# Six k-tiles of an output projection as three pairs of seven block products, in one column part of 1024

## The chip, the cores and the metric

One core of one Trainium2 chip runs one decoder layer in float32. The metric is the device time of one execution in microseconds; the median of several executions counts. TensorE is called PE in the profile, its weight loads PEld, VectorE DVE, ScalarE ACT, GpSimd POOL; SyncE (SP) only issues loads and stores.

## What is computed

A layer with 256 tokens and a model width of 2048. Two groups of eight attention heads give `mixed` (256 x 2048); the change lies in the projection that follows, and what comes behind it reads the projection's result:

```python
mixed = jnp.concatenate([a_out.reshape(B, S, DSWA_HEADS * HEAD_DIM),
                         b_out.reshape(B, S, MLA_HEADS * V_HEAD_DIM)], axis=-1)
x = x + _rmsnorm(mixed @ w_out[layer], norm_attn_post[layer])

h = _rmsnorm(x, norm_mlp_pre[layer])
u = jnp.square(jax.nn.relu(h @ w_up[layer]))
x = x + _rmsnorm(u @ w_down[layer], norm_mlp_post[layer])
```

`w_out` is 2048 x 2048, `w_up` 2048 x 8192, `w_down` 8192 x 2048.

## The kernel before

**Products of three.** A float32 operand is used as two parts, hi (rounded, made by ScalarE) and lo (the rest, made by VectorE as `source - hi`). A product is three matmuls onto one accumulator: hi x hi, hi x lo, lo x hi. The activations are the stationary side (128 x 128, one k-tile of 128 rows and one block `b` of 128 tokens), the weights the moving side, 512 columns wide. `mm` at line 304 issues them. There are NB = 2 token blocks and KD = 16 k-tiles.

**Weights.** `Weights` holds a list of weight tiles in the order of use. For each, SP loads a raw tile (up to 128 x 1024 floats, five raw buffers, line 198), then ScalarE makes hi and VectorE lo (`split`, lines 314 and 315; with a gain 318 and 319), in eight pairs of buffers. When the matmuls ask for tile i, the work for all tiles up to i + `ahead` is put out; `ahead` is 6 (`W_AHEAD`) and 4 (`AHEAD_NORM`) around the norm behind the output projection. So the order of the loads and splits in each engine's queue is fixed when the program is built.

**The order of side work.** `Flow` keeps a clock of the matmuls put out so far. Side work (norms, attention heads, evacuations) is written as generators that yield delays in microseconds; `flow.pump()` puts out what is due. `flow.until` and `flow.finish` put it out early where data are needed. Engines run their own queues in order and wait for each other by semaphores.

**The output projection.** `mixT` holds `mixed` transposed, hi and lo, k-tiles 0 to 7 from the first head group and 8 to 15 from the second. The 2048 columns are four parts of 512 (`ch_o`), each with eight weight tiles of two k-tiles. Parts 0 and 1 are interleaved, while the last heads finish; then part 2, then part 3, where the last `APART[0]` = 5 tiles (10 k-tiles) are done for token block 0 first and then for block 1. Part 2 and part 3 take 16 x 2 x 3 = 96 matmuls each. When an accumulator is complete, `out_evac` squares it on ScalarE for the norm (line 897) and multiplies it by the gain on VectorE (`yg`, line 898). At the end of parts 0 and 1 the pools of the attention are given up, the gain `g_post` and `x` are loaded, and `powers` starts: four squares of `g_post` (line 915), a few steps on 128 x 2 elements (lines 917 to 926), and four scalings of `x` (line 931).

**The residual and the next projection.** After part 3 of a token block, `residual(b)` reduces the squares, takes the root on GpSimd (line 506), updates `x` in four pieces (line 943), and transposes each piece on TensorE (`ht`, line 308); ScalarE and VectorE split it into `hT` (hi and lo). The up projection's first column part (j = 0) takes its first `APART[1]` = 7 k-tiles for block 0 and then for block 1: its 42 matmuls on block 0 lie ahead of the first that needs block 1.

**Seven products.** The later column parts of the up projection, and the down projection, already do some pairs of k-tiles otherwise. A pair of k-tiles, two token blocks and two halves of 512 columns make a 2 x 2 by 2 x 2 product of blocks, which takes eight block products of three matmuls, 24 in all; by sums of blocks it takes seven, 21 matmuls (`seven_products`). That needs, on the weights' side, two sums `t` and `u` of the pair's raw tiles on VectorE (lines 366 to 371; four adds of 512 where the two k-tiles lie in separate raw tiles), so that a pair has hi and lo of four operands, one 512 wide (`b11`) and three 1024 wide, in place of two. On the activations' side it needs four sums of blocks, split into hi and lo (`four_sums` at line 1111 does them in three instructions). Of the seven products three go straight onto the accumulators and four onto accumulators `m` of their own; after the last pair `close` (line 1175) forms what is to be added from those, by a copy on ScalarE and four VectorE instructions in a chain (line 1181), and one VectorE add for each accumulator (line 1243) ends it. `three_more` issues three matmuls onto an accumulator that such an add has changed.

Of the kernel before, what the change touches and what calls it, by code (L numbers as in the profile page):

```python
# [26 lines left out]
P = 128  # L27
D = 2048
# [48 lines left out]
APART = (5, 7)  # L77
# [37 lines left out]

THREE = up_steps(range(6, 11), (11, 12), (13,), (14, 15))
# [155 lines left out]
def layer(nc, tc, io):  # L272
    flow = Flow()

    def pool(name, side, **kw):
        return tc.alloc_tile_pool(name=name, bufs=1, side=side, **kw)
# [144 lines left out]
    wide_u, after = [], 0  # L421
# [547 lines left out]
    def heads_done(k, b):  # L969
        if k >= HA:  # L970
            flow.until(lambda: k - HA in made)
# [3 lines left out]

    res = [None] * NB
    for ns in ((0, 1), (2,), (3,)):
        if len(ns) == 2:
            order = [(c, t, b) for ts in (range(4), range(4, 6), range(6, 8)) for c in range(2) for t in ts for b in range(NB)]
        else:  # L980
            order = [(0, t, b) for t, b in in_order(8, (0, APART[0] if ns == (3,) else 0))]
        for c, b, acc in proj(mixT, [ch_o[n] for n in ns], f"o{ns[0]}", order, heads_done):
            n = ns[c]
            if not late:
                flow.finish(*workers)
                pb.release()
                lat.release()
                hp = pool("hp", "left")
                late["hT"] = [hp.tile([P, KD, S], F32R, name=f"hT_{w}") for w in ("hi", "lo")]
                po = late["po"] = pool("po", "right")  # L990
                late["g_post"] = po.tile([P, D], F32, name="g_post")
                nc.sync.dma_start(out=late["g_post"],
                                  in_=io["norm_attn_post"].partition_broadcast(P).rearrange("p o d -> p (o d)"))
                late["yg"] = [po.tile([P, D], F32, name=f"yg{b}") for b in range(NB)]
                for b_ in range(NB):
                    xs.append(po.tile([P, D], F32, name=f"x{b_}"))
                    nc.sync.dma_start(out=xs[b_], in_=io["x"][b_ * P:(b_ + 1) * P, :])
                pw_chain = flow.start(powers())
            out_evac(n, b, acc[0])
            if n == 3:  # L1000
                flow.finish(pw_chain)
                weights.ahead = AHEAD_NORM
                res[b] = flow.start(residual(b), b * D_SECOND)
                flow.pump()
# [106 lines left out]
    def four_sums(q, f):  # L1111

        tt = nc.vector.tensor_tensor
        fs, qs = [x.rearrange("p (k s) -> p k s", s=P) for x in (f, q)]
        tt(out=qs[:, 0:2], in0=fs[:, 0:2], in1=fs[:, 1:4:2], op=OP.subtract)
        tt(out=qs[:, 2], in0=qs[:, 0], in1=fs[:, 3], op=OP.add)
        tt(out=qs[:, 3], in0=fs[:, 2], in1=qs[:, 2], op=OP.subtract)

# [35 lines left out]
    def three(out, a, w, first, last):  # L1154

        for i, (x, y) in enumerate(((0, 0), (0, 1), (1, 0))):
            mm(out, a[x], w[y], first and i == 0, last and i == 2)

    def seven_products(ts, left, accs, m, first, last, m_first=False):

        (a11, a12, a22), (s3, s1, s2, s4) = left
        prods = ((a11, 0, 0, 1), (a12, 1, 0, (0, 0)), (s4, 1, 1, (0, 1)), (s2, 2, 0, 6), (a22, 2, 1, (1, 0)),
                 (s3, 3, 1, 7), (s1, 3, 0, 5))
        if m_first:
            prods = sorted(prods, key=lambda x: not isinstance(x[3], int))
        for p, (a, i, half, to) in enumerate(prods):
            w = weights.get(ts[i])
            in_m = isinstance(to, int)
            three(m[to] if in_m else accs[to], a, [w[x][:, half * 512:half * 512 + 512] for x in range(2)],
                  in_m and first, in_m and last)  # L1170
            if all(x[1] != i for x in prods[p + 1:]):
                weights.free(ts[i])
            flow.pump()

    def close(c, m):

        tt = nc.vector.tensor_tensor
        nc.scalar.activation(c[0], m[1], AF.Copy)
        for out, x, y, op in ((1, m[6], c[0], OP.subtract), (2, m[7], c[1], OP.subtract),
                              (3, m[5], c[2], OP.subtract), (1, m[5], c[1], OP.add)):  # L1180
            tt(out=c[out], in0=x, in1=y, op=op)
        return dict(zip(PARTS, c))

# [3 lines left out]
    PARTS = ((0, 0), (0, 1), (1, 0), (1, 1))  # L1187
# [121 lines left out]
    def half_evac(more, g_half):  # L1309
# [7 lines left out]
        for b, n in order:  # L1317
# [3 lines left out]
            yield 1.0  # L1321

    added = [False]

    def three_more(out, a, w):

        for x, z in ((0, 0), (0, 1), (1, 0)):
            nc.tensor.matmul(out, a[x], w[z], start=False, stop=(x, z) == (1, 0), skip_group_check=True)  # L1328
            flow.spend(MM)
# [130 lines left out]
```

## Time and profile before

| | us |
|---|---|
| median of 3 runs (lowest to highest) | 1025.0 (1021.83 to 1026.27) |
| profiled execution | 1022.25 |
| its span, first to last instruction | 1020.5 |
| PE busy in the span | 1010.1 |
| DVE, ACT, POOL busy | 839.3, 624.3, 94.0 |
| first matmul of column part 2, first of the up projection | 296.8, 341.25 |

The span is 1.75 us shorter than the execution's own time. Rows of the timeline give start, duration, engine, line, instruction, and in brackets the idle time of that engine before it with what ended it. A matmul's duration (0.39) is from its issue to its end; they overlap, so the pace is read from the starts. The row of a stage gives the busy time of each engine in it.

### The profile page before, as it was taken

How to read it: one execution, taken by the hardware profiler on the slowest of the kernel's cores; microseconds unless marked ns; L12 is line 12 of the kernel's file. 1: busy time of each engine (PE TensorE's matmuls, PEld its weight loads, DVE VectorE, ACT ScalarE, POOL GpSimd, SP SyncE). 2: the span in 40 equal slices, each digit the busy share in tenths (PEclk: the TensorE clock that was granted, in tenths of full speed). 3: DMA queues.
4: the chain of work that ended last, by engine and by line, in shares of the span. 5: the costliest groups of instructions: out<-in, count | busy, mean ns of one | idle time of the engine just before them, and what ended most of it. 6: DMA issues, size and time to landing. Idle time of an engine off the chain costs nothing.

```text
span 1020.5 us, 13280 instructions
## 1 busy us (share of the span) xinstructions
PE 1010.1 (99%) x4678; PEld 842.9 (83%) x4678; DVE 839.3 (82%) x1125; ACT 624.3 (61%) x822; POOL 94.0 (9%) x148
## 2 busy tenths in 40 slices
PE   9999999999999999999999999999999999999996
PEld 6888889898888788888888888888888888888885
DVE  6677747676656779998999989898999989898896
ACT  6575437555463567566766776676666665767571
POOL 0020202002101000000010100000110000211100
PEclk9999999999999999999999999999999999999999
DMA  8977759556686298778988979579989866988972
GB/s 291 373 253 260 251 162 313 175 165 192 201 306 210 89 385 247 259 257 242 298 258 283 286 221 301 190 254 365 344 263 385 301 226 235 326 309 293 320 258 82
DMA packets 108370, 266.02 MB, mean 261 GB/s; under 512 B 9488, under 2 KB 28432, under 8 KB 107664
## 3 DMA queue, kind: packets, MB, share of 16 engines
q1 hardware_dynamic: 65488, 177.24, 51.3%
q0 software_dynamic: 19440, 68.17, 20.3%
q10 hardware_dynamic: 23376, 19.78, 6.1%
q8 instruction: 36, 0.59, 0.2%
q14 instruction: 30, 0.25, 0.1%
HBM read 232.12 MB, written 33.03 MB: 260 GB/s over the span
## 4 chain that ended last, share of the span: by engine, by line
PE 97%; DVE 1%; issue 1%; ACT 0%; POOL 0%; DVEq 0%; POOLq 0%; ACTq 0%
PE acc_u L304 26%; PE y L304 25%; PE acc_o L304 8%; PE md L304 6%; PE m L304 6%; PE acc_v L304 5%; PE acc_qk L304 4%; PE acc_q L304 3%; PE acc_k L304 3%; PE acc_ckv L304 3%; PE acc_cq L304 2%; PE sc_b L304 1%; PE acc_qr L304 1%; PE y L1328 1%; PE sc_a L304 1%
## 5 line engine op out<-in xcount | busy, mean ns | idle before, releaser
L315 DVE TENSOR_TENSOR lo<-raw,hi 128x1024 fp32r<-128x1024 f32 (+2 forms) x205 | 233.1, 1157 | 67.6 <-ACT hi L314 66.3
L314 ACT ACTIVATE hi<-raw 128x1024 fp32r<-128x1024 f32 (+2 forms) x205 | 202.5, 1004 | 75.3 <-DMA raw<-in_w_in 19.8
L304 PE MATMUL acc_u<-hi,hT_hi 128*128 128x512 f32 x386 | 150.7, 390 | 0.1
L304 PE MATMUL acc_u<-hi,hT_lo 128*128 128x512 f32 x386 | 150.4, 390 | 0.5 <-DVE hT_lo L315 0.5
L304 PE MATMUL acc_u<-lo,hT_hi 128*128 128x512 f32 x386 | 150.2, 389 | 0.0
L304 PE MATMUL y<-lo,uhi 128*128 128x512 f32 x358 | 139.3, 389 | 0.0
L304 PE MATMUL y<-hi,ulo 128*128 128x512 f32 x358 | 139.3, 389 | 0.0
L304 PE MATMUL y<-hi,uhi 128*128 128x512 f32 x358 | 139.3, 389 | 0.0
L318 ACT ACTIVATE hi<-raw,gcol 128x1024 fp32r<-128x1024 f32 x86 | 96.9, 1148 | 36.2 <-DMA raw<-in_w_up 15.3
L319 DVE SCALAR_TENSOR_TENSOR lo<-raw,gcol,hi 128x1024 fp32r<-128x1024 f32 x86 | 106.6, 1274 | 9.4 <-ACT hi L318 9.2
L304 PEld LDWEIGHTS acc_u<-hi,hT_lo 128*128 128x128 f32 x386 | 72.5, 188 | 16.0 <-DVE hT_lo L315 0.9
L304 PEld LDWEIGHTS acc_u<-hi,hT_hi 128*128 128x128 f32 x386 | 72.5, 188 | 15.3 <-ACT hT_hi L314 0.4
L304 PEld LDWEIGHTS acc_u<-lo,hT_hi 128*128 128x128 f32 x386 | 72.5, 188 | 14.8
L304 PEld LDWEIGHTS y<-lo,uhi 128*128 128x128 f32 x358 | 67.2, 188 | 14.3 <-DVE lo L315 0.2
L304 PEld LDWEIGHTS y<-hi,ulo 128*128 128x128 f32 x358 | 67.2, 188 | 13.9
L304 PEld LDWEIGHTS y<-hi,uhi 128*128 128x128 f32 x358 | 67.2, 188 | 13.9
L315 DVE TENSOR_TENSOR lo<-st_down,hi 128x1024 fp32r<-128x1024 f32 x46 | 55.0, 1219 | 0.4 <-ACT hi L314 0.4
L304 PE MATMUL acc_o<-hi,mixT_hi 128*128 128x512 f32 x128 | 51.3, 401 | 0.0
L314 ACT ACTIVATE hi<-st_down 128x1024 fp32r<-128x1024 f32 x46 | 47.9, 1049 | 4.9 <-DVE st_down L371 2.4
L314 ACT ACTIVATE hi<-u 128x1024 fp32r<-128x1024 f32 (+1 forms) x33 | 32.2, 979 | 30.0 <-PE y L304 10.3
L304 PE MATMUL acc_o<-hi,mixT_lo 128*128 128x512 f32 x128 | 49.9, 390 | 0.0
L304 PE MATMUL md<-hi,s 128*128 128x512 f32 x138 | 49.9, 389 | 0.0
(352 smaller groups left out, 2039.7 us busy)
## 6 DMA issues: line engine op xcount, KB each, us to landing
raw<-in_w_up SPq DMA_DIRECT2D x86, 512.0 KB, 5.0
raw<-in_w_down SPq DMA_DIRECT2D x82, 512.0 KB, 6.2
raw<-in_w_in SPq DMA_DIRECT2D x55, 512.0 KB, 5.6
ab<-in_w_up POOLq DMA_DIRECT2D x17, 1024.0 KB, 7.0
raw<-in_w_out SPq DMA_DIRECT2D x32, 512.0 KB, 5.0
ab_down<-in_w_down POOLq DMA_DIRECT2D x11, 1024.0 KB, 9.7
ulo<-ukeep POOLq DMA_DIRECT2D x20, 512.0 KB, 5.9
rkeep<-r ACTq DMA_DIRECT2D x28, 256.0 KB, 3.2
```

The costliest lines, as they stand in the source:

```text
L304: nc.tensor.matmul(out, a, b, start=start, stop=stop)
L314: nc.scalar.activation(hi, src, AF.Copy)
L315: nc.vector.tensor_tensor(out=lo, in0=src, in1=hi.bitcast(F32), op=OP.subtract)
L318: nc.scalar.activation(hi, src, AF.Copy, scale=g)
L319: nc.vector.scalar_tensor_tensor(out=lo, in0=src, scalar=g, in1=hi.bitcast(F32), op0=OP.mult, op1=OP.subtract)
L1328: nc.tensor.matmul(out, a[x], w[z], start=False, stop=(x, z) == (1, 0), skip_group_check=True)
```

## The change

Column parts 2 and 3 become one part of 1024 columns, with weight tiles of one k-tile by 1024. Its k-tiles come in this order: 6, 7, 8, 9 as before; the pairs (0, 1) and (2, 3) by seven products; k-tile 10; the pair (4, 5) by seven products, those onto `m` first; then 11 to 15 as ordinary tiles. For each of the four accumulators (token block b, column half n) the tail of ordinary tiles is added onto the accumulator after the closing add: k-tile 11 is done for block 1 first, then the tail for (0, 0), (0, 1), (1, 0), (1, 1), and the evacuation and residual follow each as before. The accumulators lie in banks 4 to 7, `m` in banks 0 to 3.

The sums on the activations' side are made by `out_sums`, started when parts 0 and 1 end, in buffers of a pool `op` that is given up after the adds, before `hT` is placed. `ahead` is 3 from the last tiles of parts 0 and 1 on, and 6 again when they are done. `four_sums`, `three`, `seven_products`, `close` and `three_more` move up in the file; only `seven_products` is altered, by the argument `stop`. The diff, without what only moves:

```diff
-APART = (5, 7)
+APART = 7
...
+OUT_STEPS, OUT_LAST, AHEAD_OUT = up_steps((6, 7, 8, 9), (), (10,), ()), range(11, 16), 3
+D_LEFT = (2.0, 3.0)
...
-    ch_o = [Chunk(weights, io["w_out"], n * 512, 512, K2, plan=False) for n in range(4)]
-    for n, m in ((0, 4), (1, 4), (0, 2), (1, 2), (0, 2), (1, 2), (2, 8), (3, 8)):
+    ch_o = [Chunk(weights, io["w_out"], n * 512, 512, K2, plan=False) for n in range(2)]
+    for n, m in ((0, 4), (1, 4), (0, 2), (1, 2), (0, 2), (1, 2)):
...
+    def out_weight(k):
+        return io["w_out"][k * P:(k + 1) * P, CW:]
+
+    def seven_out(kp):
+        def load():
+            return [weights.load(out_weight(2 * kp + i), CW, f"raw_o{kp}{i}") for i in range(2)]
+
+        return seven(load, lambda: late["out_tu"])
+
+    wide_o, after = [], 0
+    for what, k in [*OUT_STEPS, *(("k", k) for k in OUT_LAST)]:
+        if what == "k":
+            ts = [weights.plan(out_weight(k), 1, CW)]
+        else:
+            ts, after = plan_seven(*seven_out(k), after, (), 0 if k else SUMS_AHEAD)
+        wide_o.append((what, k, ts))
+
...
     def heads_done(k, b):
+        if k == KD - 3:
+            weights.ahead = AHEAD_OUT
...
+    def seven_products(ts, left, accs, m, first, last, m_first=False, stop=False):
...
+            three(m[to] if in_m else accs[to], a, [w[x][:, half * 512:half * 512 + 512] for x in range(2)],
+                  in_m and first, last and (in_m or stop))
...
+    out_left = {}
+
+    def out_sums():
+
+        st = late["out_st"]
+        f, q = late["out_c"][:2]
+        yield D_LEFT[0]
+        for kp in range(3):
+            a, b = [t[:, 2 * kp:2 * kp + 2, :].rearrange("p k s -> p (k s)") for t in mixT]
+            nc.vector.tensor_tensor(out=f, in0=a.bitcast(F32), in1=b.bitcast(F32), op=OP.add)
+            four_sums(q, f)
+            o = 1024 * kp
+            split(st[:, o:o + 512], st[:, o + 512:o + 1024], q)
+            out_left[kp] = [[st[:, o + w * 512 + i * P:o + w * 512 + (i + 1) * P] for w in range(2)] for i in range(4)]
+            yield D_LEFT[1]
+
+    order = [(c, t, b) for ts in (range(4), range(4, 6), range(6, 8)) for c in range(2) for t in ts for b in range(NB)]
+    for c, b, acc in proj(mixT, ch_o, "o0", order, heads_done):
...
+            op = pool("op", "left")
+            late["out_c"], late["out_tu"] = [[op.tile([P, w], F32, name=f"out_{x}{i}") for i in range(n)]
+                                             for x, w, n in (("c", 512, 4), ("tu", CW, 2))]
+            late["out_st"] = op.tile([P, 3 * CW], F32R, name="out_st")
...
+            flow.start(out_sums())
...
+        out_evac(c, b, acc[0])
+    weights.ahead = W_AHEAD
+
+    accs = {bn: bank(4 + i, f"acc_o2_{bn[0]}{bn[1]}") for i, bn in enumerate(PARTS)}
+    n_out = len(OUT_STEPS)
+
+    def out_three(t, k, b, n, first=False, stop=False, more=False):
+        w = [x[:, 0, n * 512:n * 512 + 512] for x in weights.get(t)]
+        left = [tok(mixT[x], k, b) for x in range(2)]
+        if more:
+            three_more(accs[b, n], left, w)
+            three(accs[b, n], left, w, first, stop)
+        flow.pump()
+
+    for i, (what, k, ts) in enumerate(wide_o[:n_out]):
+        if what == "k":
+            for b, n in PARTS:
+                out_three(ts[0], k, b, n, not i)
+            weights.free(ts[0])
+            continue
+        flow.until(lambda: k in out_left)
+        if not k:
+            m = {x: bank(o, f"mo{x}") for o, x in enumerate((1, 6, 7, 5))}
+        blocks = [[tok(mixT[x], 2 * k + kk, bb) for x in range(2)] for kk, bb in ((0, 0), (1, 0), (1, 1))]
+        seven_products(ts, (blocks, out_left[k]), accs, m, not k, i == n_out - 1, i == n_out - 1, True)
+    more = close(late["out_c"], m)
+
+    def out_add(b, n):
+        nc.vector.tensor_tensor(out=accs[b, n], in0=accs[b, n], in1=more[b, n], op=OP.add)
+
+    def out_done(n, b):
+        out_evac(n + 2, b, accs[b, n])
+        if n:
+            flow.finish(pw_chain)
+            weights.ahead = AHEAD_NORM
+            res[b] = flow.start(residual(b), b * D_SECOND)
+            flow.pump()
+
+    tail_o = [(ts[0], k) for _, k, ts in wide_o[n_out:]]
+    for n in range(2):
+        out_add(0, n)
+    for n in (1, 0):
+        out_three(*tail_o[0], 1, n, stop=True, more=not n)
+    for n in range(2):
+        out_add(1, n)
+    op.release()
+    hp = pool("hp", "left")
+    late["hT"] = [hp.tile([P, KD, S], F32R, name=f"hT_{w}") for w in ("hi", "lo")]
+    for b in range(NB):
+        for n in range(2):
+            for t, k in tail_o[b:]:
+                out_three(t, k, b, n, more=True)
+                if (b, n) == (0, 1) and (t, k) == tail_o[0] or (b, n) == (1, 1):
+                    weights.free(t)
+            out_done(n, b)
...
-        order = in_order(len(steps), (APART[1], 0)) if j == 0 else [(t, b) for t, (w, _, _) in enumerate(steps)
+        order = in_order(len(steps), (APART, 0)) if j == 0 else [(t, b) for t, (w, _, _) in enumerate(steps)
```

What moves is seen in the order of the program's instructions. First VectorE, from the last yg of parts 0 and 1 on. Before, after the yg of part 1 for block 1, there stand the splits of part 2 and the powers (`gg`, `pws`, `t_pw`):

```order
L898 TENSOR_TENSOR yg_2802<-acc_o_1_1_0_2425,g_post 128x512
L315 TENSOR_TENSOR lo_2866<-raw_2863,hi_2865 128x1024
L315 TENSOR_TENSOR lo_2886<-raw_2883,hi_2885 128x1024
L315 TENSOR_TENSOR lo_2906<-raw_2903,hi_2905 128x1024
L315 TENSOR_TENSOR lo_2926<-raw_2923,hi_2925 128x1024
L917 TENSOR_REDUCE gg<-gg_2412 128x1
```

Now, between the same yg and the powers, there are (`out_tu` are the sums `t` and `u` of a pair's raw tiles `raw_o`, `out_c` the sums of the activations' blocks, `out_st` their lo) these rows, and behind them, still ahead of the powers, the third left sum and the second pair's four sums and first two splits:

```order
L917 TENSOR_TENSOR yg_2805<-acc_o_1_1_0_2425,g_post 128x512
L317 TENSOR_TENSOR lo_2871<-raw_2868,hi_2870 128x1024
L371 TENSOR_TENSOR out_tu_2796<-raw_o_2759 128x512
L371 TENSOR_TENSOR out_tu_2796<-raw_o_2759,raw_o_2761 128x512
L372 TENSOR_TENSOR out_tu_2797<-out_tu_2796,raw_o_2761 128x512
L373 TENSOR_TENSOR out_tu_2797<-out_tu_2797,raw_o_2761 128x512
L317 TENSOR_TENSOR lo_2879<-raw_o_2759,hi_2878 128x512
L317 TENSOR_TENSOR lo_2883<-raw_o_2761,hi_2882 128x1024
L317 TENSOR_TENSOR lo_2887<-out_tu_2797,hi_2886 128x1024
L317 TENSOR_TENSOR lo_2905<-out_tu_2796,hi_2904 128x1024
```

Of the four splits of ordinary tiles ahead of the powers one is left; in place of the other three stand the sums and splits of two pairs. Two of the three left sums stand ahead of this yg, the third behind it.

The second place is VectorE at the end of the part, where in before the yg of the last part's block 0 followed three splits for the up projection. Now these rows come ahead of it:

```order
L317 TENSOR_TENSOR lo_3104<-raw_3101,hi_3103 128x1024
L317 TENSOR_TENSOR lo_3113<-raw_3110,hi_3112 128x1024
L317 TENSOR_TENSOR lo_3119<-raw_3116,hi_3118 128x1024
L1034 TENSOR_TENSOR out_c_2793<-mo_2979,out_c_2792 128x512
L1034 TENSOR_TENSOR out_c_2794<-mo_2980,out_c_2793 128x512
L1034 TENSOR_TENSOR out_c_2795<-mo_2981,out_c_2794 128x512
L1034 TENSOR_TENSOR out_c_2793<-mo_2981,out_c_2793 128x512
L1109 TENSOR_TENSOR acc_o_00_2864<-acc_o_00_2864,out_c_2792 128x512
L1109 TENSOR_TENSOR acc_o_01_2865<-acc_o_01_2865,out_c_2793 128x512
```

The splits of all tail tiles (11 to 15) stand ahead of the close and of the adds onto the accumulators. On TensorE, the place where the tail begins:

```order
L306 MATMUL acc_o2_11_2867<-hi120_3072,mixT_lo_80 128x512
L1040 MATMUL acc_o2_10_2866<-hi120_3072,mixT_hi_79 128x512
L1040 MATMUL acc_o2_10_2866<-lo120_3073,mixT_hi_79 128x512
L1040 MATMUL acc_o2_10_2866<-hi120_3072,mixT_lo_80 128x512
L1040 MATMUL acc_o2_00_2864<-hi120_3072,mixT_hi_79 128x512 [waits DVE_49]
L1040 MATMUL acc_o2_00_2864<-lo120_3073,mixT_hi_79 128x512
```

The matmuls of k-tile 11 (tile 120) on block 1 stand last ahead of the tail; the tail's first matmul, on `acc_o2_00`, waits (`DVE_49` is VectorE's semaphore) for the add onto that accumulator. From there to the up projection there are 54 matmuls, as many as in before from the same distance; block 1's last ones, behind block 0's last, are 24 where they were 30.

More of the change, by code (lines that the diff above doesn't have):

```diff
@@ L974, in h_done @@
         flow.until(lambda: 4 * parts[b] > k)
-    res = [None] * NB
-    for ns in ((0, 1), (2,), (3,)):
-        if len(ns) == 2:
-            order = [(c, t, b) for ts in (range(4), range(4, 6), range(6, 8)) for c in range(2) for t in ts for b in range(NB)]
-        else:
[L981 to L1004, printed above, removed]
@@ L1152, in all_sums @@
         yield from left_sums(2)
[L1154 to L1182, printed above, removed]
     def closing():
         return [late["c"][:, i * 512:(i + 1) * 512] for i in range(4)]
-    PARTS = ((0, 0), (0, 1), (1, 0), (1, 1))
     evac = []
@@ L1323, in layer @@
     added = [False]
[L1325 to L1329, printed above, removed]
     hp.release()
```

53 lines of the change are left out of this document (46 added, 7 removed).

## The prediction

> **What bounds the kernel now.** I read the page's table of engines first, then what TensorE (PE) waits for, then the stretch in which the change lies.
>
> ```profile
> PE 1010.1 (99%) x4678; PEld 842.9 (83%) x4678; DVE 839.3 (82%) x1125; ACT 624.3 (61%) x822; POOL 94.0 (9%) x148
> ```
> ```profile
> PE warm L527 <- DVE zero L524: 1.2, 1, 1.2
> PE acc_u L304 <- DVE hT_lo L315: 0.5, 1, 0.5
> ```
> TensorE is busy for 1010.1 of 1020.5 us, and the view of its waits has two rows in all, 1.7 us together. So it is the bound everywhere, and a matmul less is a gain only while nothing else becomes late. The chain of waits gives a matmul's pace, the view of stages the room that the other engines have (columns: stretch, its length, then PE, PEld, DVE, ACT, POOL busy):
>
> ```profile
> 281.97 56.47 PE acc_o L304 x249
> ```
> ```profile
> 290.00:341.00 51.00, 51.00 (x230) 42.26 (x229) 30.31 (x42) 24.56 (x40) 4.12 (x7) 1.00 0.63 203
> ```
> 249 matmuls in 56.47 us are 0.2268 us each. In the 51 us of this stage VectorE (DVE) is busy for 30.3, so 20.7 are free. That is the figure to set the change against.
>
> **What it takes off TensorE.** Three pairs of k-tiles cost 3 x 24 matmuls before and 3 x 21 now: 9 x 0.2268 = 2.04 us. The program's row count on PE falls by the same 9, so it does what it says.
>
> **What it puts on VectorE.** The timelines give the price of each kind of instruction; I take the step from one start to the next, which is what a queue costs:
>
> ```profile
> 404.88 1.22 DVE L315 TENSOR_TENSOR lo<-u,hi 128x1024 fp32r<-128x1024 f32 x1
> 406.02 1.22 DVE L315 TENSOR_TENSOR lo<-t,hi 128x1024 fp32r<-128x1024 f32 x1
> 407.15 1.22 DVE L366 TENSOR_TENSOR t<-ab 128x1024 f32<-128x1024 f32 x1
> 408.41 0.69 DVE L370 TENSOR_TENSOR u<-t,ab 128x512 f32<-128x512 f32 x1
> 409.13 0.69 DVE L371 TENSOR_TENSOR u<-u,ab 128x512 f32<-128x512 f32 x1
> 409.74 1.28 DVE L319 SCALAR_TENSOR_TENSOR lo<-raw,gcol,hi 128x1024 fp32r<-128x1024 f32 x1
> ```
> A full-width lo costs 1.14. The sums of a pair of weight tiles cost 1.26 + 0.72 + 0.61 = 2.59 (here they are four adds of 512 in place of one of 1024 and two of 512; the same elements, so the same price). A half-width lo is 512 elements like the last add: 0.61.
>
> The Trainium skill, "VectorE: DVE Perf Modes", section "The TRN2 errata", prices an fp32 add of N elements at (N + 151)/0.96 ns. That is 1.22 and 0.69 us, the durations in these rows; but where nothing holds an instruction back the next one starts 0.08 earlier. By the page the queue below would be some 2 us longer; I go by the starts.
>
> For the sums of the left side, the two products' closing adds and the small steps, rows from the up and down projections and from this stage:
>
> ```profile
> 390.96 0.69 DVE L1127 TENSOR_TENSOR c<-hT_hi,hT_lo 128x512 f32<-128x512 f32 x1
> ```
> ```profile
> 723.99 0.68 DVE L315 TENSOR_TENSOR s<-st_down,s 128x512 fp32r<-128x512 f32 x1
> ...
> 732.50 0.42 DVE L1115 TENSOR_TENSOR st_down<-uT 128x256 f32<-128x256 f32 x1
> 732.95 0.29 DVE L1116 TENSOR_TENSOR st_down<-st_down,uT 128x128 f32<-128x128 f32 x1
> 733.28 0.29 DVE L1117 TENSOR_TENSOR st_down<-uT,st_down 128x128 f32<-128x128 f32 x1
> ```
> ```profile
> L314 ACT ACTIVATE s<-st_down 128x512 fp32r<-128x512 f32 x14 | 8.8, 632 | 43.5 <-DVE st_down L1117 25.9 <-PE md L304 8.9 <-PE y L304 4.9
> ```
> ```profile
> 305.32 0.15 DVE L917 TENSOR_REDUCE gg<-gg 128x1 f32<-128x4 f32 x1
> 305.50 0.23 DVE L918 TENSOR_SCALAR pws<-ss,gg 128x2 f32<-128x2 f32 x1
> 305.77 0.17 DVE L505 TENSOR_SCALAR t_pw<-pws 128x2 f32<-128x2 f32 x1
> ...
> 307.39 0.16 DVE L921 TENSOR_SCALAR pw<-rstd_pw 128x2 int32<-128x2 int32 x1
> ...
> 308.21 0.75 DVE L931 TENSOR_SCALAR x<-x,pw 128x1024 f32<-128x1024 f32 x1
> 308.97 1.23 DVE L315 TENSOR_TENSOR lo<-raw,hi 128x1024 fp32r<-128x1024 f32 x1
> ```
> ```profile
> 423.91 2.87 DVE L1181 TENSOR_TENSOR c<-m,c 128x512 f32<-128x512 f32 x4
> 426.70 2.47 DVE L319 SCALAR_TENSOR_TENSOR lo<-raw,gcol,hi 128x1024 fp32r<-128x1024 f32 x2
> 429.09 2.49 DVE L1243 TENSOR_TENSOR acc_u<-acc_u,c 128x512 f32<-128x512 f32 x4
> ```
> One left sum is 0.69 + 0.42 + 0.29 + 0.29 on VectorE, then 0.63 on ScalarE, for which VectorE's queue stands still, then 0.68: 3.00, and 0.17 for the hand-overs (0.03 to 0.05 each, as between these rows): 3.17. The steps of the powers are 0.62 and 0.82, each scaling of x 0.76. The close is 426.70 - 423.91 = 2.79, an add onto an accumulator 0.69.
>
> **Where the two engines meet.** Everything up to the second yg stands as before. In before that yg, and the first matmul of column part 2, are:
>
> ```profile
> 292.33 0.69 DVE L898 TENSOR_TENSOR yg<-acc_o,g_post 128x512 f32<-128x512 f32 x1 [0.68 <-ACT junko L897]
> ```
> ```profile
> 296.79 0.39 PE L304 MATMUL acc_o<-hi,mixT_hi 128*128 128x512 f32 x1
> ```
> VectorE is free again at 292.95. From there its queue, in the order that the program gives it, runs:
> - two left sums with the two other yg between them: 2 x 3.17 + 2 x 0.62, and some 0.3 (an estimate, from the matmuls that the third yg still needs) of waiting: 300.8
> - lo of k-tile 9: its hi stands on ScalarE behind the fourth square, which now stands behind the second left sum's split (300.2 + 1.05 + 0.1); with 1.14: 302.5
> - first pair: sums 2.59, a half lo 0.61, three lo 3.42: 309.1
> - third left sum: 312.3
> - second pair, with 0.62 of the powers: 319.5 (its half lo at 315.5)
> - third pair's sums, lo of k-tile 10: 323.3
> - powers 0.82, four scalings of x 3.04, half lo 0.61, three lo 3.42, and the lo of the five tail k-tiles 5.70: 336.8
> - close 2.79, first add 0.69: 340.3
>
> TensorE's order up to the tail is 48 + 21 + 21 + 12 + 21 + 6 = 129 matmuls, so without a wait it would be at the tail at 296.79 + 129 x 0.2268 = 326.05. The tail's first matmul adds onto acc_o(0,0) and waits for VectorE's first add: 340.3. TensorE is already held before that: the second pair's first lo is there at 315.5 and would be read at 312.7, k-tile 10's and the third pair's follow the same way. These waits change nothing in the sum, since the last one ends at 340.3 in any case: VectorE hardly waits for TensorE in this stretch. Before, the same point of the tail (54 matmuls ahead of the end) was reached at 296.79 + 138 x 0.2268 = 328.1. So the stage ends 340.3 - 328.1 = 12.2 us later, the nine matmuls included.
>
> **After the tail.**
>
> ```profile
> 333.77 0.60 ACT L897 ACTIVATE junko<-acc_o 128x512 bf16<-128x512 f32 x1 [5.71 <-PE acc_o L304]
> ...
> 338.28 0.60 PE L308 MATMUL ht<-ident,x 128*128 128x128 f32 x4
> ...
> 339.54 0.69 DVE L315 TENSOR_TENSOR hT_lo<-ht,hT_hi 128x512 fp32r<-128x512 f32 x1 [1.22 <-ACT hT_hi L314]
> ...
> 341.25 0.39 PE L304 MATMUL acc_u<-hi,hT_hi 128*128 128x512 f32 x1
> ```
> Token block 0's residual needs 340.23 - 333.77 = 6.46 us from its last matmul to hT_lo. Block 1's matmuls that cover it were 30 (6.8 us) and are now 24 (5.4 us, and 0.45 for the transposes), and hT_lo is read 0.45 later: some 0.3 of a wait is new. Block 1's residual keeps its cover of 42 matmuls of the up projection; VectorE's queue there has the same instructions in a slightly other order, and I put 0.2 on that. Loads, buffers and queues after this are as before, and TensorE, being the bound there, has nothing with which to catch up.
>
> Sum: 12.2 + 0.3 + 0.2 = 12.7 us. The profiled execution took 1022.25, so 1035.0 on its scale; the median of the three runs shown, 1025.0, lies 2.75 above it, which gives 1037.7. I forecast 1036.
>
> Below that price the queue could come out shorter if ScalarE's part of the left sums were partly hidden and every hand-over were free: 3 us at most, from the 3 x 0.80 and the 0.6 of waiting above. Nothing takes it longer by much but the cases below.
>
> **Rivals.**
>
> *VectorE keeps up.* The 20.7 free microseconds and the loads ahead absorb it, TensorE never waits, and only the nine matmuls remain: 1022.25 - 2.0 = 1020.2. It decides where the queue from 292.95 to the first add takes under 33.1 us (326.05 - 292.95) in place of 47.4. Against it: the change adds 28 us (three full and three half lo more, 5.3; three pairs' sums, 7.8; three left sums, 9.5; close and four adds, 5.3) where 20.7 are free, and the last of these were free because the buffers ahead were full. 5 in 100.
>
> *TensorE comes back slow.* The last wait lasts about 5 us, after shorter ones. How TensorE runs after standing still is seen in before only at its start:
>
> ```profile
> 1.19 3.60 PE L527 MATMUL warm<-zero 128*128 128x512 bf16 x8 [1.19 <-DVE zero L524]
> ...
> 6.99 0.39 PE L304 MATMUL acc_qk<-hi,xT_hi 128*128 128x512 f32 x1
> ```
> The first eight take 0.45 each, twice the pace, and the steady pace is there by 6.99. If that comes again, 3.6 to 5.8 us run at half pace, in a tail where TensorE is the bound: 1.8 to 2.9 us lost, 1036.8 to 1037.9 on the profiled scale, 1038.4 as forecast is counted. 25 in 100. The Trainium skill, "TensorE: Matmul & The Clock Gate", section "Part 1: The HAM clock gate", has such a rule: an idle window of about 3.4 us halves the clock until a busy one has passed. No row of before shows it in mid-program; the granted clock there stays at 1.00.
>
> *A load ends last.* The tail's last weights are fetched into the raw buffer that the third pair's second tile leaves, at 327.4.
>
> ```profile
> DMA to landing us min/median/max: 3.5/5.5/13.1
> ```
> At the median they are there before their turn; at 13.1 the hi is done at 341.6, the lo at 342.8 and the first add at 346.3, 6 us later than above: 1041.0 on the profiled scale. 7 in 100.
>
> **Numbers.** The forecast has 58 in 100; 5 are left for a smaller loss that I can't name. A measurement of this kernel can tell about 0.5%, 5.1 us, from no change. Slower by more than that are the forecast, the slow return and the late load, and most of the unnamed: 0.91. The case in which VectorE keeps up gains 0.2%, so it counts as the same: 0.07 with the rest; faster by over 0.5% has no mechanism: 0.02. The range: from 1030 (the queue 3 us shorter, 1032.0, less 2 for the spread of the runs, which reach 3.2 below their median) to 1041 (the slow return, or a late load, from the median).
>
> **What will show it.** Right, if VectorE is busy nearly without a gap from 293 to 340, if TensorE waits for lo at the second and third pair, and if the longest wait is on the first accumulator add, near 340. Wrong, if TensorE goes through the tail without a wait, if it waits there for a load, or if the loss lies in the up projection. The step I trust least is the price of a left sum, which stands three times.

## The result and the profile after

The changed kernel takes 1038.3 us (median of 6 runs, 1036.22 to 1041.01), the kernel before 1023.9 (6 runs, 1021.83 to 1026.27): 14.4 us more, ratio 1.0134 with a 95% interval of [1.0118, 1.0149] (later ratios have theirs in brackets too). The forecast was 1036.0, the range 1030 to 1041. The profiled execution took 1038.36 with a span of 1036.5.

The first part of the page of after (busy time, share, instructions) has the nine matmuls fewer, 4669 for 4678, and VectorE 23.5 us busier:

```profile
PE 1015.0 (98%) x4669; PEld 842.6 (81%) x4669; DVE 862.8 (83%) x1166; ACT 631.4 (61%) x832; POOL 95.4 (9%) x148
```

TensorE's waits in after (us in total, times, the longest). Before had two, 1.2 and 0.5; the first three here are new (two more of 0.6 each, not shown, lie outside the stage):

```profile
PE acc_o L1040 <- DVE acc_o L1109: 4.9, 1, 4.9
PE mo L306 <- DVE lo L317: 3.1, 2, 2.2
PE acc_o L306 <- DVE lo L317: 2.1, 2, 1.9
...
PE acc_u L306 <- DVE hT_lo L317: 0.4, 1, 0.4
```

VectorE's timeline of after: the second yg, the third left sum with the first instruction behind it, the close and the first two adds:

```profile
293.22 0.69 DVE L917 TENSOR_TENSOR yg<-acc_o,g_post 128x512 f32<-128x512 f32 x1 [0.68 <-ACT junko L916]
...
309.61 0.69 DVE L1053 TENSOR_TENSOR out_c<-mixT_hi,mixT_lo 128x512 f32<-128x512 f32 x1
...
312.11 0.69 DVE L317 TENSOR_TENSOR out_st<-out_c,out_st 128x512 fp32r<-128x512 f32 x1 [0.70 <-ACT out_st L316]
312.72 0.68 DVE L371 TENSOR_TENSOR out_tu<-raw_o 128x512 f32<-128x512 f32 x1
...
336.74 2.87 DVE L1034 TENSOR_TENSOR out_c<-mo,out_c 128x512 f32<-128x512 f32 x4
339.52 1.29 DVE L1109 TENSOR_TENSOR acc_o<-acc_o,out_c 128x512 f32<-128x512 f32 x2
```

A left sum takes 312.72 - 309.61 = 3.11, as priced (3.17). TensorE's timeline of after has the waits on the second pair's first lo and on k-tile 10's, the wait on the first accumulator add, and what follows it:

```profile
315.99 0.50 PE L306 MATMUL mo<-lo,mixT_hi 128*128 128x512 f32 x1 [2.23 <-DVE lo L317]
...
323.71 0.50 PE L306 MATMUL acc_o<-lo,mixT_hi 128*128 128x512 f32 x1 [1.91 <-DVE lo L317]
...
340.27 0.79 PE L1040 MATMUL acc_o<-hi,mixT_hi 128*128 128x512 f32 x1 [4.87 <-DVE acc_o L1109]
340.86 0.63 PE L1040 MATMUL acc_o<-lo,mixT_hi 128*128 128x512 f32 x1
...
345.85 0.39 PE L1040 MATMUL acc_o<-lo,mixT_hi 128*128 128x512 f32 x1
```

From 340.27 to 345.85 there are 13 matmuls; at 0.2268 they would take 2.95, and they took 5.58: 2.63 us are lost to a slower pace, 0.427 each. The windows of after (busy us of PE, PEld, DVE, ACT and POOL, then the granted clock, DMA share, GB/s) show the clock beside it:

```profile
293.00:340.00 47.00, 37.27 (x151) 28.53 (x149) 43.35 (x67) 26.09 (x40) 5.01 (x6) 0.95 0.47 162
340.00:345.00 5.00, 4.73 (x11) 3.76 (x12) 5.00 (x7) 1.05 (x1) 0.00 (x0) 0.50 0.63 215
```

From 340 to 345 the granted clock is 0.50. And from 293 to 340 VectorE is busy for 43.35 of 47 us; of the 3.65 left, 2.1 are the waits of 0.70 for ScalarE inside the three left sums.

**The balance.** The stage begins 0.89 later in this execution (the second yg at 293.22; 292.33 before), so I count from that yg's end, 0.61 behind its start. The same point of the tail is, in the timeline of before:

```profile
328.07 0.39 PE L304 MATMUL acc_o<-hi,mixT_hi 128*128 128x512 f32 x1
```

Before: 328.07 - 292.94 = 35.13. After: 340.27 - 293.83 = 46.44. That is 11.31 later, and 2.63 of slow matmuls make 13.9 of the 14.4 us. (The two profiled executions differ by 16.1: 0.9 lies ahead of the second yg and 1.2 far behind the stage. Executions of one kernel differ by as much.)

### The profile page after: what moved, and what is told of

It is laid out like the page before. It is cut to its first block, busy times and chain, and to the rows that moved or that the text cites. A ratio compares the mean times of both kernels' runs of the same rounds, so it can differ in the third digit from the quotient of the medians.

```text
span 1036.5 us, 13316 instructions
## 1 busy us (share of the span) xinstructions
PE 1015.0 (98%) x4669; PEld 842.6 (81%) x4669; DVE 862.8 (83%) x1166; ACT 631.4 (61%) x832; POOL 95.4 (9%) x148
## 4 chain that ended last, share of the span: by engine, by line
PE 89%; DVE 5%; DMA 3%; issue 1%; ACT 1%; POOL 0%; DVEq 0%; SPq 0%; POOLq 0%; ACTq 0%
PE acc_u L306 26%; PE y L306 23%; PE m L306 6%; PE acc_v L306 5%; PE md L306 5%; PE acc_o L306 4%; PE acc_qk L306 4%; PE acc_k L306 3%; PE acc_q L306 3%; PE acc_ckv L306 2%; DVE lo L317 2%; PE acc_cq L306 2%; DMA ab_down<-in_w_down 1%; PE acc_o L1040 1%; PE sc_b L306 1%
## 5 line engine op out<-in xcount | busy, mean ns | idle before, releaser
L317 DVE TENSOR_TENSOR lo<-raw,hi 128x1024 fp32r<-128x1024 f32 (+2 forms) x199 | 225.7, 1156 | 61.9 <-ACT hi L316 60.7
L316 ACT ACTIVATE hi<-raw 128x1024 fp32r<-128x1024 f32 (+2 forms) x199 | 196.0, 1002 | 71.2 <-DMA raw<-in_w_in 25.2
L306 PEld LDWEIGHTS y<-hi,ulo 128*128 128x128 f32 x358 | 67.2, 188 | 13.9
L306 PEld LDWEIGHTS y<-hi,uhi 128*128 128x128 f32 x358 | 67.2, 188 | 13.9
L317 DVE TENSOR_TENSOR lo<-u,hi 128x1024 fp32r<-128x1024 f32 (+1 forms) x33 | 36.5, 1118 | 5.3 <-ACT hi L316 5.3
L316 ACT ACTIVATE hi<-ab 128x512 fp32r<-128x512 f32 (+1 forms) x36 | 30.0, 841 | 17.8 <-PE acc_u L306 13.6
```

The source lines that it names most:

```text
L306: nc.tensor.matmul(out, a, b, start=start, stop=stop)
L316: nc.scalar.activation(hi, src, AF.Copy)
L317: nc.vector.tensor_tensor(out=lo, in0=src, in1=hi.bitcast(F32), op=OP.subtract)
```

## The experiments

The theory: VectorE's queue in the stage, by its amount of work, sets when the tail starts, and the clock's slow return comes on top. The rivals: a fixed cost of the closing chain however many pairs there are, and the order in which close and adds stand behind the tail's lo's. All kernels are edits of the changed one.

### How many pairs

In no_pair all k-tiles are ordinary, and the four adds are gone with the close:

```diff
-OUT_STEPS, OUT_LAST, AHEAD_OUT = up_steps((6, 7, 8, 9), (), (10,), ()), range(11, 16), 3
+OUT_STEPS, OUT_LAST, AHEAD_OUT = up_steps((6, 7, 8, 9, 0, 1, 2, 3, 4, 5, 10)), range(11, 16), 3
...
-            flow.start(out_sums())
...
-    more = close(late["out_c"], m)
```

one_pair has `up_steps((6, 7, 8, 9, 2, 3, 4, 5, 10), ())` there, two_pairs `up_steps((6, 7, 8, 9, 4, 5), (10,), ())`, and `out_sums` makes one or two left sums:

```diff
-        for kp in range(3):
+        for kp in range(2):
```

> The wide column part stays, all sixteen k-tiles are ordinary, without left sums, products, close and adds. Theory (the loss is the amount of work that the pairs put on VectorE's queue): 138 matmuls up to the tail again, VectorE keeps up, the time of before within 1.5 us: 1024, no wait of TensorE over 1 us in the stage. Rival (the wide part itself costs: loads, buffers, the order of block 0 and block 1 in its tail): several microseconds above before, 1027 or more.

1024.42 against 1024.39 for before, ratio 1.0001 [0.9983, 1.0019], and no wait over 0.5 us in the stage. The wide part costs nothing: all of the loss comes with the pairs.

> Two pairs. Theory: VectorE's first add comes 7.5 us sooner than with three, near 332.7, TensorE is there at 327.6: a wait of about 5 us in all, 3.8 us above before (1027.7), and up to 2 more if the slow matmuls after the wait come again (1029.7). Rival with a fixed cost: as one pair. Rival with a cost in proportion to the pairs (no slack on VectorE at all): two thirds of 14.4, 1033.5.

1030.41, ratio 1.0051 [1.0031, 1.0072], 6.0 us above before. The tail starts 332.19 - 293.25 = 38.94 after the second yg. The theory had 46.44 - 7.5 = 38.9; the nine matmuls behind it lost 1.9 to the slow pace.

> One pair by seven products in place of three, with the same close and adds. Theory: two pairs less take 15 us off VectorE's queue (each 3.17 + 2.59 + 0.61 + 3.42 less 2 x 1.14 for the two ordinary lo's), so its first add comes near 325 where TensorE gets there at 328: no wait, 0.7 us of matmuls saved, 1023.5. Rival (a fixed cost: the products in banks of their own and the closing chain that the tail waits on, however many pairs): the wait stays, 6 us or more above before, 1030 or more.

1029.40, ratio 1.0048 [1.0032, 1.0064], 5.0 above before where the theory had none. Here it fails. TensorE, VectorE and ScalarE in one_pair:

```profile
323.82 0.39 PE L306 MATMUL mo<-hi,out_st 128*128 128x512 f32 x1
...
331.18 0.80 PE L1040 MATMUL acc_o<-hi,mixT_hi 128*128 128x512 f32 x1 [3.57 <-DVE acc_o L1109]
```
```profile
308.02 1.23 DVE L317 TENSOR_TENSOR lo<-raw,hi 128x1024 fp32r<-128x1024 f32 x1 [4.61 <-ACT hi L316]
...
323.11 4.62 DVE L317 TENSOR_TENSOR lo<-raw,hi 128x1024 fp32r<-128x1024 f32 x4
327.65 2.87 DVE L1034 TENSOR_TENSOR out_c<-mo,out_c 128x512 f32<-128x512 f32 x4
330.44 1.29 DVE L1109 TENSOR_TENSOR acc_o<-acc_o,out_c 128x512 f32<-128x512 f32 x2
```
```profile
306.93 1.06 ACT L316 ACTIVATE hi<-raw 128x1024 fp32r<-128x1024 f32 x1 [4.72 <-DMA raw<-in_w_out]
```

VectorE has the time, but not when it could use it: it stands for 4.61 us because ScalarE's hi waits for a load. Then comes the rest of its queue, with hardly a gap. The last product onto `m` ends by 324.2, and from there TensorE has 15 matmuls, 3.4 us, up to the tail's wait; VectorE has the tail's four lo's, the close and an add, 331.05 - 323.11 = 7.9. So with one pair a cost is left that does not go with the number of pairs, as in the rival, which had 6 us or more. The closing chain, 3.4 us by itself, has 3.4 us of cover, and what stands in front of it on VectorE is waited for. Without the 4.61 us the first add would be done at 331.05 - 4.61 = 326.4 (an estimate), ahead of TensorE, which is there at 327.6: the late load is enough to make this wait, and that the chain costs something by itself is not shown.

### The standstill's own cost

```diff
+    fill = bank(0, "fill")
+    for _ in range(18):
+        nc.tensor.matmul(fill, zero[:, :P], zero, start=True, stop=True)
     op.release()
```

> The changed kernel with 18 matmuls on zeros (bf16, into a free bank) where TensorE stands still before the accumulator add; nothing else is touched, and VectorE's queue does not depend on it. Theory of the slow return (the standstill lowers the granted clock, and the 13 matmuls at 0.427 behind it cost 2.6 us): the add comes when it did, the tail runs at 0.227, 2 to 2.6 us faster than the changed kernel, 1036. Rival (the slow matmuls have another cause, or their time is hidden): no change, 1038.3, the same 13 matmuls at 0.427.

1035.23, ratio 1.0104 [1.0078, 1.0131], against 1.0134 of the changed kernel: 3 us less. TensorE in fill:

```profile
315.34 0.53 PE L306 MATMUL mo<-lo,mixT_hi 128*128 128x512 f32 x1 [2.23 <-DVE lo L317]
315.68 0.62 PE L306 MATMUL mo<-hi,mixT_lo 128*128 128x512 f32 x1
...
334.55 4.06 PE L1128 MATMUL fill<-zero 128*128 128x512 bf16 x17
339.62 0.50 PE L1040 MATMUL acc_o<-hi,mixT_hi 128*128 128x512 f32 x1 [1.01 <-DVE acc_o L1109]
339.95 0.40 PE L1040 MATMUL acc_o<-lo,mixT_hi 128*128 128x512 f32 x1
```

The tail starts 46.44 after the second yg (292.57 + 0.61), exactly as in after, and then runs at 0.23. So VectorE's queue sets the start of the tail, and the standstill costs its 2.6 us apart from that. (The slow matmuls that begin at 315.68 are hidden: TensorE waits for VectorE again behind them.)

### Less on VectorE, or in another order

late_x puts the four scalings out by a function called behind the adds; late_lo keeps the lo's of k-tiles 12 to 15 back (`held`), puts them out behind the first two adds, and sets `ahead` to 5 for the last pair; in pool_left and pool_pairs `four_sums` and `seven` are told the engine of their adds.

```diff
-        for b in range(NB):
-            for c in (slice(0, CW), slice(CW, D)):
-                nc.vector.tensor_scalar_mul(xs[b][:, c], xs[b][:, c], pw[:, b:b + 1])
-                yield 1.5
...
+    scale_x()
     op.release()
```
```diff
     for n in range(2):
         out_add(0, n)
+    for f in weights.held:
+        f()
```
```diff
-            nc.vector.tensor_tensor(out=f, in0=a.bitcast(F32), in1=b.bitcast(F32), op=OP.add)
-            four_sums(q, f)
+            nc.gpsimd.tensor_tensor(out=f, in0=a.bitcast(F32), in1=b.bitcast(F32), op=OP.add)
+            four_sums(q, f, nc.gpsimd)
```
```diff
-        return seven(load, lambda: late["out_tu"])
+        return seven(load, lambda: late["out_tu"], nc.gpsimd)
```

> The changed kernel with the four scalings of x (0.76 us each) moved on VectorE's queue from the middle of the stage to behind the last accumulator add, where VectorE has time. Theory (with three pairs VectorE's queue sets when the tail starts): the first add comes 2.3 to 3.0 us sooner (the lower figure if the last tail tile's load, whose hi starts at 332.2, ends ahead of the queue), so 1035.7; with fewer slow matmuls behind the shorter wait as low as 1033. Rival (loads or the closing chain set it, and VectorE's amount does not): no change, 1038.3.

1034.89, ratio 1.0105 [1.0086, 1.0124]. The tail starts 337.98 - 294.02 = 43.96 after the second yg, 2.5 sooner than in after.

> The changed kernel with the lo of k-tiles 12 to 15 put on VectorE's queue behind the first two adds in place of ahead of the close. The amount of work is the same. Theory: the first add comes at 337.2 in place of 340.2 (ScalarE's copy of the first product, at 333.7, holds the close from then on), but the four lo's, 1.14 each, then stand between the adds and the tail's matmuls, which take 0.68 per k-tile, and give 1 to 2.3 back: 1035 to 1037.5. Rival (the cause is the place of the close behind the tail's lo's): 4.6 us sooner and no slow matmuls, 1031 to 1033.

1035.57, ratio 1.0111 [1.0096, 1.0126]. The adds come 337.95 - 293.63 = 44.32 after the yg, 2.1 sooner, and a lo is the next to be waited for, in the timeline of TensorE:

```profile
339.67 0.50 PE L1052 MATMUL acc_o<-lo,mixT_hi 128*128 128x512 f32 x1 [0.53 <-DVE lo L323]
```

This order moves the loss by 2 to 3 us; the rival's 1031 to 1033 did not come. VectorE stands for 1.97 us in front of the close here, for ScalarE's copy, which stands behind the hi of the last tail tile and its load. What the order would give without that no run shows.

> The changed kernel with the four adds of each of the three left sums on GpSimd (3 x 1.69 us of VectorE); the lo of each, 0.69, stays on VectorE behind ScalarE's hi. Theory: 5.1 us less on VectorE's queue, and up to 2.4 more if VectorE has other work ready while GpSimd and ScalarE are at it, though its queue is in order: 1031 to 1033.5. Rival: VectorE stands still for GpSimd's longer adds at the same places, and nothing is gained: 1037 or more.

1032.49, ratio 1.0083 [1.0067, 1.0098]. The tail starts 335.13 - 292.99 = 42.14 after the yg, 4.3 sooner than in after; 5.1 had been taken off VectorE.

> The changed kernel with the sums of the weight pairs (twelve adds of 128x512, 7.8 us on VectorE) on GpSimd. No run shows GpSimd's price of such an add. Theory: VectorE's queue is 7.8 us shorter if GpSimd takes at most about twice VectorE's time per add, and the time falls by 5 to 8 us, to 1030.5 to 1033. Rival (the sums on GpSimd take longer than the loads run ahead, or slow VectorE down where both read): the lo's of the sums wait for GpSimd and VectorE's queue stands behind them: between 1036 and slower than the changed kernel.

1037.63, ratio 1.0130 [1.0110, 1.0149]: nothing gained, as the rival had it. The tail starts 47.38 after the yg though VectorE has 7.8 us less to do. GpSimd's and VectorE's timelines in pool_pairs:

```profile
321.76 1.28 POOL L371 TENSOR_TENSOR out_tu<-raw_o,raw_o 128x512 f32<-128x512 f32 x1
323.01 1.28 POOL L372 TENSOR_TENSOR out_tu<-out_tu,raw_o 128x512 f32<-128x512 f32 x1
```
```profile
320.57 1.26 DVE L940 TENSOR_SCALAR pw<-rstd_pw 128x2 int32<-128x2 int32 x1
321.86 1.21 DVE L941 TENSOR_SCALAR pwi<-pw 128x2 int32<-128x2 int32 x1
323.11 1.21 DVE L942 TENSOR_SCALAR pwi<-pwi 128x2 f32<-128x2 f32 x1
...
325.65 0.74 DVE L950 TENSOR_SCALAR x<-x,pw 128x1024 f32<-128x1024 f32 x1
```

The powers' steps on 128 x 2 elements, 0.16 to 0.17 in before, take 1.21 to 1.26 here, each as long as the GpSimd add beside it; together 325.65 - 320.57 = 5.1 for 0.82. The three small sums in the third left sum go the same way, 1.26 to 1.39 each for 0.29 to 0.42, and make it 6.5 long for 3.1. That is 7.7 us, and the gain is gone.

The Trainium skill, "GPSIMD Engine Reference", section "8. Key points", says that GpSimd shares its SBUF interfaces with VectorE and contends with some of its instructions, and section "4.1 Engine selection" that elementwise work with two inputs is about twice as slow there. Both agree with these rows (1.28 for what takes VectorE 0.69). In the rows an instruction of VectorE that is short by itself lasts as long as a whole one of GpSimd beside it.

### Away with the last wait

mid_add puts the adds behind block 0's k-tiles 11 to 13. `limit` holds the splits for the up projection back until then (tiles counted from the oldest in use):

```diff
+    weights.limit = len(tail_o)
     for n in (1, 0):
         out_three(*tail_o[0], 1, n, stop=True, more=not n)
+    for n in range(2):
+        for t, k in tail_o[:3]:
+            out_three(t, k, 0, n, more=True)
+    for b, n in PARTS:
+        out_add(b, n)
+    weights.limit = W_BUFS
...
-            for t, k in tail_o[b:]:
+            for t, k in tail_o[1 if b else 3:]:
```

two_mid is two_pairs with this and late_x's edit, three_all the changed kernel with this, late_x's and pool_left's.

> The changed kernel with the accumulator adds 18 matmuls later: block 0's k-tiles 11 to 13 run ahead of the adds, its last two behind them. VectorE's queue is the same up to the adds. Theory: TensorE gets to the first add 18 x 0.2268 = 4.1 us later, at 339.3, where the add is done at 340.2: of the wait of 4.9 us 0.9 is left, and the slow matmuls behind it (2.6 us) go with it: 1031.6; if TensorE's clock falls behind the earlier, shorter waits instead, 1034. What is left over before is then the waits on the lo's of the second and third pair, 6 us. Rival (what the adds cost comes back at the end, where block 0's residual starts later): 1036 or more.

1034.93, ratio 1.0119 [1.0096, 1.0142]; the theory had 1031.6. The wait on the adds is gone, and two others have come, as TensorE's waits in mid_add from 280 to 385 show:

```profile
PE mo L306 <- DVE lo L317: 4.4, 3, 2.2
PE acc_u L306 <- DVE hT_lo L317: 1.6, 1, 1.6
PE ht L310 <- DVE x L962: 1.1, 1, 1.1
PE acc_o L306 <- DVE lo L317: 0.8, 1, 0.8
```

The clock fell as well: it is 0.50 for 3.41 us from 317.61, from 331.26 and from 355.16, behind waits on lo's and on hT_lo. That is the expectation's second case, with 1034.

> Two pairs, the scalings of x behind the adds, and the adds 18 matmuls later. Theory: VectorE's first add comes near 329, TensorE is there at 331.2; no wait is left in the stage, six matmuls (1.4 us) are saved, and 0.3 is lost in the residual: 1.0 us below before, ratio 0.999. Rival (another cost of the products that the waits have hidden so far): 2 us or more above before, ratio 1.002 or more.

1029.88, ratio 1.0067 [1.0044, 1.0090]; the theory had 0.999, the rival 1.002 or more. In two_mid TensorE does not wait before the residual, where it waits for `x`. TensorE's waits from 280 to 385 and VectorE's timeline:

```profile
PE ht L310 <- DVE x L963: 3.8, 1, 3.8
PE acc_u L306 <- DVE hT_lo L317: 1.1, 1, 1.1
```
```profile
334.65 2.73 DVE L952 TENSOR_SCALAR x<-x,pw 128x1024 f32<-128x1024 f32 x4
337.30 3.67 DVE L321 SCALAR_TENSOR_TENSOR lo<-raw,gcol,hi 128x1024 fp32r<-128x1024 f32 x3
340.89 1.28 DVE L917 TENSOR_TENSOR yg<-acc_o,g_post 128x512 f32<-128x512 f32 x2
...
343.23 1.41 DVE L963 SCALAR_TENSOR_TENSOR x<-yg,rstd_post,x 128x512 f32<-128x512 f32 x2 [0.70 <-POOL rstd_post L525]
```

The work that I moved out of the adds' way (2.65) and three splits for the up projection (3.59) now stand ahead of block 0's yg, and so ahead of its update and transposes. My expectation counted 0.3 for this place.

> Three pairs with the left sums' adds on GpSimd, the scalings of x behind the adds, and the adds 18 matmuls later. Theory: with the left sums away the waits on the lo's of the second and third pair come to 3 us in all, less up to 2 for the scalings, and no other wait is left: 1.0 us below to 1.5 above before less 2.0 for nine matmuls, about as before, ratio 0.998 to 1.002. Rival (slow matmuls behind the short waits, or GpSimd in VectorE's way): ratio 1.004 or more.

1030.10, ratio 1.0062 [1.0050, 1.0074], again in the rival's range (1.004 or more), and the loss lies at the same place as in two_mid. Waits before the residual are down to 1.5 in all, and `ht` waits for `x` for 3.2.

two_fit is two_pairs with mid_add's edit, with block 1's scalings of x alone moved, and with the up projection's splits let in one by one:

```diff
+    weights.limit = len(tail_o) + 1
...
             out_done(n, b)
+        weights.limit += 1
...
+            if b:
+                list(scale_x(b))
             res[b] = flow.start(residual(b), b * D_SECOND)
```

> Two pairs, the adds 18 matmuls later, block 0's scalings of x where they were, block 1's two moved behind block 1's last yg, and the up projection's weight splits let in one at a time so that block 0's residual (yg, update, hT_lo) does not stand behind three of them on VectorE. Theory (what is left of the loss is only what stands ahead on VectorE's queue where TensorE waits for it): the first add ends near 332, when TensorE is there; block 0's update ends near 340, where its transposes are due; six matmuls (1.4 us) are saved and 0.5 is lost in short waits: 1 us below before, ratio 0.998 to 1.001. Rival (seven products cost something here that no order of VectorE's queue takes away): ratio 1.003 or more.

1027.42, ratio 1.0039 [1.0025, 1.0053]: the best of the kernels with pairs, 2.5 us less than two_mid, and still slower than before, by an amount that the rival had (1.003 or more). What is left is again a wait for VectorE's queue. TensorE's longest wait from 280 to 385 and VectorE's timeline in two_fit:

```profile
PE ht L310 <- DVE hT_lo L317: 2.6, 1, 2.6
```
```profile
343.83 3.67 DVE L321 SCALAR_TENSOR_TENSOR lo<-raw,gcol,hi 128x1024 fp32r<-128x1024 f32 x3
347.42 0.75 DVE L965 SCALAR_TENSOR_TENSOR x<-yg,rstd_post,x 128x512 f32<-128x512 f32 x1
348.08 0.69 DVE L317 TENSOR_TENSOR hT_lo<-ht,hT_hi 128x512 fp32r<-128x512 f32 x1
```

Of the four pieces of block 0's update three are in time now; the fourth, and the second hT_lo, stand behind three splits. Whether an order exists in which nothing is waited for stays open. Two pairs could save six matmuls, 1.4 us, which is less than a measurement of this kernel tells from no change.

The profiled executions of two_mid and two_fit are the slowest of their runs, 6.0 and 4.0 us above the medians. Each has a wait of 3.0 or 3.1 us far behind the stage (near 970 and 967, in the down projection), for a lo whose load is late. No_pair has 0.6 there and is no slower than before, so I don't count this wait to the change; why the load is late no run shows.

### The account

For the kernels whose tail waits for the adds: the stretch from the second yg's end to the first matmul behind the adds, less 35.13; the slow matmuls right behind it (their time less 0.2268 each, up to where the pace is steady again); the sum; and the difference of the medians from before.

| kernel | stretch | later than before | slow matmuls | sum | medians |
|---|---|---|---|---|---|
| after | 46.44 | 11.3 | 2.6 | 13.9 | 14.4 |
| fill | 46.44 | 11.3 | 0 | 11.3 | 10.8 |
| pool_pairs | 47.38 | 12.3 | 1.7 | 14.0 | 14.0 |
| late_lo | 44.32 | 9.2 | 2.7 | 11.9 | 12.0 |
| late_x | 43.96 | 8.8 | 1.7 | 10.5 | 11.3 |
| pool_left | 42.14 | 7.0 | 1.7 | 8.7 | 8.9 |
| two_pairs | 38.94 | 3.8 | 1.9 | 5.7 | 6.0 |
| one_pair | 38.18 | 3.1 | 1.6 | 4.7 | 5.0 |

Two terms give every row within 0.8 us (late_lo's second holds its wait for a lo as well). The matmuls saved are in the stretch.

The other kernels can be counted from the second yg's end to one and the same matmul of the up projection (at 375.02 in before; it and all behind it are 2809 instructions on TensorE). They take longer than before by the figures below, within 1.3 us of the medians. So the loss lies ahead of that matmul in each of them:

| kernel | to that matmul | medians |
|---|---|---|
| no_pair | 0.0 | 0.0 |
| after | 14.0 | 14.4 |
| mid_add | 11.6 | 11.7 |
| two_mid | 5.3 | 6.6 |
| three_all | 6.7 | 6.8 |
| two_fit | 2.9 | 3.4 |

## Why the prediction was right

- **Nine matmuls.** 4669 for 4678. They are not seen in the time: TensorE waits in that stretch.
- **VectorE's queue.** Predicted 47.4 from the second yg to the first add, measured 46.4. The single prices held: a left sum 3.11 for 3.17, the close 2.78 for 2.79. The step that I trusted least was sound. late_x, pool_left and two_pairs took work off this queue and moved the tail by 2.5, 4.3 and 7.5; fill left the queue alone and did not move it.
- **The earlier waits "change nothing in the sum".** True while the last one is there: fill's slow matmuls at 315.68 cost nothing. In mid_add, with the last wait away, 5.2 us of them come to light.
- **The place.** Predicted first add near 340, a lo of the second pair waited for from 312.7 to 315.5; measured 340.2, and a wait of 2.23 that ends at 315.99. That 340 was hit so closely is in part luck: the stage began 0.9 later in this execution, and the queue was 1.0 shorter.
- **What was too small.** The forecast's 1036 took nothing for the clock after the wait. TensorE coming back slow was a rival of its own, with 25 in 100, priced at 1.8 to 2.9 us and 1038.4. It came, with 2.63 and 1038.3, and fill shows it to be the cause of its part. So the forecast's sum had the right mechanism and lacked one term. Of its 12.7 us, 0.9 of the stage and 0.5 after the tail did not come, and 2.6 of slow clock did: 13.9. That the rival's 1038.4 is so near 1038.3 is in part luck, since it holds the 1.4 that did not come. (Where the prediction says "twice the pace" of matmuls of 0.45, it is twice the time.)
- **After the tail.** 0.3 and 0.2 were put there. hT_lo is waited for 0.4 in all, as in before (0.5). Nothing was lost there in after; it is where the loss goes once the adds are out of the way.
- **VectorE keeps up, a late load.** Neither came with three pairs. A load did come late in one_pair, where it was VectorE that stood still for it.

The Trainium skill, "TensorE: Matmul & The Clock Gate", section "Part 1: The HAM clock gate", has the clock halved after an idle window of about 3.4 us, in windows that run freely. The wait of 4.87 and the 0.50 behind it agree. But in fill the clock is low from 315.68 on, behind a wait of only 2.23 with dense matmuls ahead of it, and in after the same wait of 2.23 at 315.99 has no slow matmul behind it. The granted clock in narrow windows of after settles the second point:

```profile
325.21:328.62 3.41, 3.41 (x10) 2.60 (x8) 3.41 (x5) 1.95 (x3) 0.05 (x1) 0.50 0.72 238
328.62:338.80 10.18, 5.95 (x25) 4.17 (x23) 9.97 (x12) 5.00 (x6) 2.57 (x4) 1.00 0.73 227
338.86:345.69 6.83, 5.42 (x13) 4.26 (x14) 6.72 (x9) 1.41 (x2) 0.00 (x0) 0.50 0.71 243
```

The changes lie whole multiples of 3.41 us apart: 325.21, 328.62, 338.86 (3 further), 345.69 (2 further). Going back on the same grid, a border at 314.97 cuts the wait of 2.23 in after into 1.21 and 1.02, and the clock stays at 1.00; the wait of 1.91 that ends at 323.71 lies whole between 321.79 and 325.21, and at 325.21 the clock falls. In fill the wait of 2.23 lies whole in the 3.41 us that end at 315.68.

## What to carry to other kernels

Price a change that takes work from the bounding engine by the queue of the engine that gets work in its place: from the last point where that engine is free, in the program's order, to the first place where the bounding engine reads the result, and not by its idle share of the stage. Idle time that an earlier load or a full buffer makes cannot be used by work that stands behind it. Add what the clock loses after the standstill, and when a wait is moved away, ask who stands next behind the same queue: here it was the residual.

## What the runs showed of the hardware

- The slow pace is 0.427 a matmul, at a granted clock of 0.50. In each trace the clock changes only at times that lie whole multiples of 3.41 us apart. Between 290 and 360, in the changed kernel and the kernels with pairs, it fell 20 times, each time at the end of such a window of 3.41 us in which TensorE stood for 1.64 us or more (48%, in mid_add); it never fell behind one with 1.62 or less (47%, in fill). It rose again behind a window with 0.35 or less, and stayed low behind those with 1.09 or more. So what a standstill costs in clock depends on where it lies in the windows: two_pairs and after wait 4.9 us before the tail, and have 9 and 13 slow matmuls behind it. Some 17 matmuls on zeros in the gap (4.06 us) kept the clock up.
- A VectorE instruction of 0.16 us takes 1.2 us while GpSimd works through adds of 128 x 512, and GpSimd's first such add there took 2.21 in place of 1.28. In pool_left GpSimd's adds are done by 300.6, and behind that VectorE's prices are as in after.
